# Two-layer encoder step: attention loads tied to older stores, output weights' splits spread wider, the second layer's first tile normed without a fixed place

## The chip, the cores and the metric

The kernel runs on one core of a Trainium2 chip. The metric is the device time of one execution in microseconds (us). The core has TensorE (PE: matmuls; its weight loads are shown as PEld), VectorE (DVE), ScalarE (ACT), GpSimd (POOL) and SyncE (SP), which here issues nearly all DMA transfers, in its own program order. Each engine works through its instructions in order and waits on semaphores for what the others and the DMAs produce.

## The reference

The input is 2048 prompt tokens and 64 sample tokens of width 1024. Layer A: RMS norm, one projection to q, k, v and gate, softmax attention in a band of 64-token chunks (own chunk and eight before it, learned bias), times SiLU(gate), output projection, residual. Layer B: keys and values from one projection of the stream behind layer A, q and gate from another, stick-breaking attention over all earlier keys, and the same output step; a last norm ends it. The sample tokens attend to caches as well. Cut to what matters:

```python
# layer A
q, k, v, gate = split(rms_norm(x, g_a) @ w_in_a)
x = x + (band_attend(q, k, v, rel_bias) * silu(gate)) @ w_out_a
# layer B
k, v = split(rms_norm(x, g_kv) @ w_kv)
q, gate = split(rms_norm(x, g_b) @ w_in_b)
log_fail = where(mask, log_sigmoid(-z), 0)           # z = q k^T * scale
later = reverse_cumsum(log_fail) - log_fail
w = where(mask, exp(log_sigmoid(z) + later), 0)
x = x + ((w @ v) * silu(gate)) @ w_out_b
y = rms_norm(x, g_f)
```

All in fp32, with 16 heads of 64, taken as 8 head pairs (hp).

## The kernel before, in words

Every fp32 product is three matmuls: each operand is split in a high and a low part (ACT writes the rounded high part, DVE the rest: `split`), and high x high, high x low and low x high are summed. Nearly all compute instructions go through one helper, so the profile shows them as L89 and they are told apart by their tiles.

**Stages**, in us of the profiled execution: layer A's v projection 0 to 216, its k, q and gate projections to 725, its attention to 1331, the last output tiles to 1430; layer B's v projection to 1638, its k, gate and q projections to 2036, its attention to 3191, the last output tiles to the end at about 3295.

**Projections.** `projections` norms a token tile (`turned`: load `xt`, sum of squares on ACT, `ms` on DVE, `rstd` on POOL, scaling, then eight transposes on PE to `ps_tr`), splits it to `x_own`, and multiplies it with the split v weights (`vraw` to `vwh`, `vwl`). The first two tiles and the first weights of a layer are traced with `order.on` set: then every instruction gets an edge to the one traced before it on its engine, so its place is fixed there. The others are placed by a scheduler that runs a simulated timeline over the dependences.

**What attention reads.** q, k, v and gate lie in DRAM scratch (`q_a`, `k_a`, `v_a`, `gate_a`, and `_b`). `load_q` (L475), `load_gate` (L485), `load_k` (L491), `load_v` (L500) and the `Sample` class (L516, the sample tokens' own loads `qs`, `gs`, `kt`, `vt`) issue on SyncE, as do the band bias `bias` (L1076) and the sample's `bs` (L1136). A finished block of attention output is gated and stored to `o_a` or `o_b` (L584).

**Beats and side work.** Attention runs by beats (`Beat`, L840): a beat starts one score tile (scores, softmax or stick-breaking on ACT, DVE and POOL), transposes the weights of an earlier one to `wt`, splits them to `ph` and `pl`, and multiplies an older block with the values (`acc`). Beside that the projections and output tiles that were put off are worked in steps: each beat adds a rate to an account (0.4 in A, 0.3 in B), and while it holds 1.0 or more a step runs and its cost is taken off: 1.0 for a step with matmuls, 0.5 for one without. The side work in order: late jobs (`late_job`, L701: the second half of the tokens' k, q or gate of a head pair; four in A, sixteen in B; the result `sp` or `sg` is stored in pieces, and for k rows `lkn` adds the parts back and `token_rows` transposes them by `ps_r` to the output); eight steps that load and split the output weights (`w_out_steps`, L752: `woraw` to `big`, a step without matmuls, with two splits on ACT and two on DVE); then 17 output tiles (`out_tile`: load `og` and `xr`, split to `oh` and `ol`, matmuls to `ps_o`, add, store of the new residual stream). `sp`, `sg`, `lkn` and `xr` share two buffers, so a new one waits for the stores out of the older one. What side work is left when attention ends runs alone.

**What sets the order of the loads.** SyncE issues in the order that the scheduler gives it. Loads for attention are traced well ahead of their use, and the scheduler places each when its simulated time finds its buffer free. A DMA can also wait for the landing of the one that was issued eight before it.

Of the kernel before, what the change touches and what calls it, by code (L numbers as in the profile page):

```python
# [16 lines left out]
P = 128  # L17
# [3 lines left out]
DH = 64  # L21
# [78 lines left out]
def encoder_step(ctx: ExitStack, tc: tile.TileContext, a: dict, o: dict):  # L100
# [105 lines left out]
    def put(L, kind, hp, s, cols, part):  # L206

        for i in (0, 2) if kind == "q" and s == 0 else (s,):
            nc.sync.dma_start(f32(lay[L][kind][hp][i, :, cols]), f32(part))


    def projections(L, x_of, begin, w_v, cv, gv, out_v, jobs, first, prompt, sample, stages):
        with (
# [262 lines left out]
    def load_q(L, pool, hp, h, q0):  # L476

        there(L, "q", hp, q0)
        q = pool.tile([P, 2, CH], F32R, name="q", tag="q", bufs=3 if L == "a" else 2)
        src = f32(lay[L]["q"][hp][:, h * DH : h * DH + DH, place(q0) : place(q0) + CH]).rearrange("s d t -> d s t")  # L480
        for s in range(2):
            nc.sync.dma_start(f32(q[s * DH : s * DH + DH]), src[:, s : s + 2])
        return q

    def load_gate(L, pool, hp, q0):  # L485
        there(L, "g", hp, q0)
        gt = pool.tile([P, CH], F32, name="gt", tag="gt", bufs=2)
        nc.sync.dma_start(gt, lay[L]["g"][hp][:, place(q0) : place(q0) + CH])
        return gt

    def load_k(L, hp, k0, kt):  # L491

        there(L, "k", hp, k0)
        c = place(k0) if k0 < T else k0
        for s in range(2):
            src = f32(lay[L]["k"][hp][s, :, c : c + kt.shape[2]])
            nc.sync.dma_start(f32(kt[s * DH : s * DH + DH]), src.rearrange("(h d) t -> d h t", h=2))

    def load_v(L, pool, hp, k0, n, bufs):

        tag = "vn" if n == P else "vs" if bufs == 1 else "vt"
        vt = pool.tile([P, n // P, 2, P], F32R, name="vt", tag=tag, bufs=2 if n == P else bufs)
        nc.sync.dma_start(
            f32(vt), f32(lay[L]["v"][k0 : k0 + n, 2 * hp : 2 * hp + 2]).rearrange("(j p) h c -> p j h c", p=P)
        )
        return vt
# [6 lines left out]
    class Sample:  # L513
# [9 lines left out]
        def queries(self, hp):  # L523
            q = self.q[hp % 3]
            for h in range(2):
                rows = slice(h * DH, h * DH + DH)
                src = f32(lay[self.L]["q"][hp][0:2, rows, NEW : NEW + NS])
                nc.sync.dma_start(f32(q[rows, :, rows]), src.rearrange("s d t -> d s t"))
            return q

        def gate(self, pool, hp):
            gt = pool.tile([P, NS], F32, name="gs", tag="gs", bufs=2)
            nc.sync.dma_start(gt, lay[self.L]["g"][hp][:, NEW : NEW + NS])
            return gt

        def keys_values(self, pool, hp, k0, n, bufs):
            kt = pool.tile([P, 2, n], F32R, name="kt", tag="kn" if n == NS else "kt", bufs=2 if n == NS else bufs)
            c = place(k0) if k0 < T else k0
            nc.sync.dma_start(f32(kt), f32(lay[self.L]["k"][hp][:, :, c : c + n]).rearrange("s p t -> p s t"))
# [16 lines left out]
    def gate_steps(L, pool, acc, h, c0, n, gt, sums, hp, g):  # L556
# [12 lines left out]
        def close():  # L569
            ot, tmp = sums["ot"], sums.pop(h)  # L570
            if L == "a" and n > NS:
                gps.tensor_tensor(ot[mine, :n], ot[mine, :n], tmp[mine, :n], ALU.add)
            else:
                dve.tensor_tensor(ot[mine, :n], acc()[mine, c0 : c0 + n], tmp[mine, :n], ALU.add)
            if h == 0:
                return
            if L == "b":

                t0, m = g * (CH // P), max(n // P, 1)
                by = ot[:, :n].rearrange("p (t q) -> p t q", t=m)  # L580
# [109 lines left out]
    def late_job(L, kind, w, c0, g, hp, x2, first, prompt):  # L690
# [23 lines left out]
        def out(c):  # L714
            ps = st["ps"]
            at = slice(place(HALF + c), place(HALF + c) + CH)
            if kind == "g":
                sg = opool.tile([P, CH], F32, name="sg", tag="xr", bufs=2)
                act.activation(sg, ps, AF.Sigmoid)
                dve.tensor_tensor(sg, ps, sg, ALU.mult)  # L720
                nc.sync.dma_start(lay[L]["g"][hp][:, at], sg)
            else:
                sp = opool.tile([P, 2, CH], F32R, name="sp", tag="xr", bufs=2)
                split(sp[:, 0], sp[:, 1], ps)
                for s in range(2):
                    put(L, kind, hp, s, at, sp[:, s])
                st[c] = sp
            if c + CH == HALF:
                done_late.add((L, kind, hp))
# [6 lines left out]
        def token_rows(c):  # L736
# [7 lines left out]
            nc.sync.dma_start(dst.rearrange("(j p) c -> p j c", p=P), kn[:, 1].rearrange("p (j c) -> p j c", j=4))  # L744

        chunks = range(0, HALF, CH)
        behind = []
# [92 lines left out]
    class Beat:  # L840
# [1 line left out]

        def __init__(self, lag, hold, scores_first):
            self.lag, self.hold, self.scores_first = lag, hold, scores_first
# [16 lines left out]
        def step(self):  # L863
# [60 lines left out]
        def beat(self, first=None):  # L924
# [43 lines left out]
        def end(self):  # L968
            self.rate = 1.0
            while self.tiles or self.blocks or self.held or self.marks:  # L970
                self.beat()
            order.amid = False
            while self.now or self.beside:
                self.ready = 0
                self.step()
# [47 lines left out]
    with (  # L1023
# [6 lines left out]
        banks.update(ph=4)  # L1030
        new = Sample("a", wpool)
        w_out = []
        beat = Beat(LAG["a"], HOLD["a"], True)
        beat.beside = job_steps("a", jobs_a, x2, NP - CACHE_A, o["a_k_p"])
        beat.beside += w_out_steps(a["w_out_a"][0], w_out)
        order.on = False

        def done_a(t, n, xr, c):
            if c:
                nc.sync.dma_start(x1_rows(t), xr[:n])  # L1040

        def soft_max(b, out, z, s):

# [18 lines left out]
        def items():  # L1062
            for part in ORDER:
                for hp in range(HP):
                    c0, vs = max(min(part) - 1, 0), {}
                    keys = pool.tile([P, 2, SEEN * CH], F32R, name="keys", tag="keys", bufs=2)
                    for g in part:
                        sums = {}
                        for h in range(2):
# [3 lines left out]
                                load_k("a", hp, c * CH, keys[:, :, (c - c0) * CH : (c - c0 + 1) * CH])  # L1073
                            if h == 0 and g == part[0]:
                                bias = pool.tile([P, 2, 640], F32, name="bias", tag="bias", bufs=2)
                                nc.sync.dma_start(bias, biasd[hp])  # L1076
# [52 lines left out]
        def sample_item(hp):  # L1129
            st, sums = {}, {}  # L1130

            def one():

                bs = pool.tile([P, 576], F32, name="bs", tag="bs", bufs=1)
                for h in range(2):
                    nc.sync.dma_start(bs[h * DH : h * DH + DH], biasd[hp][0:DH, h, 0:576])  # L1136
# [62 lines left out]
    with (  # L1199
# [281 lines left out]
```

## Time and profile before

| what | value |
|---|---|
| three runs | 3301.7, 3307.01, 3307.56 us (median 3307.01) |
| profiled execution | 3303.79 us |
| its span, first to last instruction | 3301.9 us |
| busy time DVE | 1922.0 us (58%) |
| busy time ACT | 1730.6 us (52%) |
| busy time POOL | 1296.1 us (39%) |
| DMA traffic | 644.37 MB, mean 195 GB/s |
| largest PE group, `ps_t<-x_own,wh` | 569.2 us of 2304 matmuls |
| `wt<-ident,s` on PE | 551.7 us of 3472 matmuls |
| `pl<-wt,ph` on DVE | 549.5 us of 864 |

A row of a timeline gives the start, the duration, the engine, the operation, what is written from what, the count, and in brackets how long the engine sat idle before it and who ended that. For a DMA the engine is SPq, and the duration is that of issuing; the landing is later. A row of stretches gives from:to, the length, the busy time of each engine with its count of instructions, the granted TensorE clock (1.00 is full), the DMA engines' share and GB/s. A piece of the chain is a start, a length and what was waited for.

### The profile page before, as it was taken

What the parts mean: (1) busy time and instruction counts of PE and PEld (TensorE: products, weight loads), DVE (VectorE), ACT (ScalarE), POOL (GpSimd) and SP (SyncE); (2) the same over time, 40 slices, a digit from 0 to 9 for tenths busy, and PEclk for the clock granted to TensorE, in tenths of its full rate; (3) what the DMA queues carried; (4) which work ended last, traced back from release to release, by engine and by line L of the source; (5) the groups of instructions that cost most, each with busy time, mean ns of one, the idle gap of its engine ahead of it and who ended that gap; (6) DMA issues with size and microseconds to landing.
All of it is one profiled execution on the core that took longest, in us unless ns stands there. A gap on an engine that the chain in (4) does not pass through costs nothing.

```text
span 3301.9 us, 53682 instructions
## 1 busy us (share of the span) xinstructions
PE 3215.2 (97%) x17928; PEld 2796.8 (85%) x17928; DVE 1922.0 (58%) x3882; ACT 1730.6 (52%) x3815; POOL 1296.1 (39%) x1950
## 2 busy tenths in 40 slices
PE   9999999999999999999999999999999999999999
PEld 7889999988888898878889999788878877888877
DVE  4234431117787777232044333899888888888873
ACT  5223322227897777143133432666666666666662
POOL 3001120005575554021044200444467776777761
PEclk9999999999899999999999999999999999999999
DMA  6359994258889894554399857777634564455423
GB/s 205 115 197 348 343 342 144 91 172 257 238 244 246 228 256 139 171 169 140 105 352 354 287 186 224 204 204 195 192 103 132 155 190 132 123 149 142 131 82 118
DMA packets 459195, 644.37 MB, mean 195 GB/s; under 512 B 49845, under 2 KB 272085, under 8 KB 458918
## 3 DMA queue, kind: packets, MB, share of 16 engines
q1 hardware_dynamic: 399462, 589.80, 57.9%
q10 hardware_dynamic: 59456, 51.13, 4.8%
q8 instruction: 143, 2.34, 0.3%
q14 instruction: 134, 1.10, 0.1%
HBM read 389.90 MB, written 250.90 MB: 194 GB/s over the span
## 4 chain that ended last, share of the span: by engine, by line
PE 77%; DVE 8%; issue 5%; DMA 4%; ACT 3%; POOL 2%; SPq 1%; POOLq 0%; DVEq 0%; ACTq 0%
PE ps_t L89 25%; PE ps_v L89 11%; PE acc L89 10%; PE ps_o L89 8%; PE z L89 8%; PE wt L89 8%; PE ps_j L89 5%; DVE s L89 3%; DVE pl L89 2%; PE ps_tr L89 1%; DVE lwl L89 1%; ACT ph L89 1%; ACT s L89 1%; POOL s L89 1%; PE ps_c L89 1%
## 5 line engine op out<-in xcount | busy, mean ns | idle before, releaser
L89 DVE TENSOR_TENSOR pl<-wt,ph 128x512 fp32r<-128x512 f32 (+1 forms) x864 | 549.5, 653 | 104.3 <-ACT ph L89 101.4
L89 ACT ACTIVATE ph<-wt 128x512 fp32r<-128x512 f32 (+1 forms) x864 | 483.2, 577 | 200.4 <-PE wt L89 191.3
L89 PE MATMUL ps_t<-x_own,wh 128*128 128x362 f32 (+1 forms) x2304 | 569.2, 327 | 0.0
L89 PE MATMUL wt<-ident,s 128*128 128x128 f32 x3472 | 551.7, 276 | 9.5 <-DVE pl L89 6.1
L89 PEld LDWEIGHTS wt<-ident,s 128*128 128x128 f32 x3472 | 421.7, 142 | 84.1 <-DVE pl L89 10.1
L89 ACT ACTIVATE f<-z 128x512 f32<-128x512 f32 (+4 forms) x680 | 355.8, 536 | 191.0 <-PE z L89 123.4
L89 POOL TENSOR_TENSOR s<-f,s 128x256 f32<-128x256 f32 x416 | 358.6, 864 | 125.7 <-DVE s L89 118.0
L89 PEld LDWEIGHTS ps_t<-x_own,wh 128*128 128x128 f32 x2304 | 405.2, 188 | 2.2
L89 PE MATMUL acc<-ph,vt 128*128 128x512 f32 (+3 forms) x1088 | 376.5, 381 | 11.4 <-ACT ph L89 5.7
L89 PE MATMUL acc<-pl,vt 128*128 128x512 f32 (+3 forms) x1088 | 367.1, 371 | 19.3 <-DVE pl L89 18.2
L89 PE MATMUL z<-kt,q 128*128 128x512 f32 (+3 forms) x1280 | 371.7, 378 | 9.6 <-ACT f L89 9.2
L89 PE MATMUL ps_t<-x_own,wl 128*128 128x362 f32 (+1 forms) x1152 | 376.6, 327 | 0.0
L89 POOL TENSOR_SCALAR s<-s,rc 128x640 f32<-128x640 f32 (+5 forms) x264 | 194.8, 744 | 427.8 <-DMA keys<-k_a 250.7
L89 PE MATMUL ps_o<-big,oh 128*128 128x512 f32 x1088 | 337.9, 394 | 0.8 <-ACT oh L89 0.5
L89 DVE TENSOR_TENSOR_SCAN s<-two,s,own 128x256 f32<-128x256 f32 x408 | 298.6, 736 | 37.8 <-POOL two L89 28.4
L89 POOL TENSOR_TENSOR two<-f 128x256 f32<-128x256 f32 x416 | 261.9, 632 | 119.6 <-ACT f L89 108.6
L89 PE MATMUL ps_t<-big,wh 128*128 128x512 f32 x896 | 278.4, 391 | 0.0
L89 PEld LDWEIGHTS z<-kt,q 128*128 128x128 f32 x1280 | 221.4, 190 | 39.9 <-ACT f L89 16.7
L89 PEld LDWEIGHTS acc<-pl,vt 128*128 128x128 f32 x1088 | 196.1, 192 | 58.8 <-DVE pl L89 44.1
L89 PEld LDWEIGHTS ps_o<-big,oh 128*128 128x128 f32 x1088 | 203.0, 189 | 42.9 <-ACT oh L89 0.9
L89 PEld LDWEIGHTS acc<-ph,vt 128*128 128x128 f32 x1088 | 198.9, 192 | 35.5 <-ACT ph L89 11.5
L89 PEld LDWEIGHTS ps_t<-x_own,wl 128*128 128x128 f32 x1152 | 216.3, 188 | 0.1
(148 smaller groups left out, 5585.0 us busy)
## 6 DMA issues: line engine op xcount, KB each, us to landing
vt<-v_b SPq DMA_DIRECT2D x80, 512.0 KB, 4.9
v_b<-vs SPq DMA_DIRECT2D x64, 512.0 KB, 5.5
q<-q_a SPq DMA_DIRECT2D x128, 256.0 KB, 5.8
q<-q_b SPq DMA_DIRECT2D x128, 256.0 KB, 4.2
vt<-v_a SPq DMA_DIRECT2D x48, 512.0 KB, 7.6
kt<-k_b SPq DMA_DIRECT2D x96, 256.0 KB, 6.2
keys<-k_a SPq DMA_DIRECT2D x80, 256.0 KB, 6.9
v_a<-vs ACTq DMA_DIRECT2D x32, 512.0 KB, 2.6
```

Source lines behind the costliest of these rows:

```text
L89: ins = op(*args, **kwargs)
```

## The change

It has three parts, and no arithmetic is changed.

1. **A queue for attention's loads.** A class `Queue` with a pace of 24 notes the attention's stores (the blocks of `o`, the late jobs' gate, q and k pieces, their token rows, and the new residual stream) with the beat in which each was traced. A load traced through it gets an edge that lets it be issued only after the newest store that is at least 24 beats old. The list is cleared when a layer's attention ends.
2. **The steps without matmuls cost more**: 1.5 in layer A and 1.0 in layer B instead of 0.5, so the eight weight steps take some 30 and 27 beats instead of some 10 and 13.
3. **The second layer's first tile**: its load and norm are traced before `order.on` is set, so their places are free; its transposes keep theirs.

```diff
+    class Queue:
+        def __init__(self, pace):
+            self.pace, self.clock, self.stores = pace, 0, []
+
+        def store(self, out, in_):
+            self.stores.append((self.clock, nc.sync.dma_start(out, in_)))
+
+        def load(self, out, in_):
+            while len(self.stores) > 1 and self.stores[1][0] <= self.clock - self.pace:
+                self.stores.pop(0)
+            behind = self.stores and self.stores[0][0] <= self.clock - self.pace
+            with tc.issue_after(self.stores[0][1].ins) if behind else nullcontext():
+                nc.sync.dma_start(out, in_)
+
+        def clear(self):
+            self.clock, self.stores = 0, []
+
+    queue = Queue(24)
...
-                def turned(t, scale=gps.tensor_scalar):
+                def normed(t, scale=gps.tensor_scalar):
                     r0, n = TOK[t]
...
                     scale(xt[:n], xt[:n], r[:n], 1.0, ALU.mult, ALU.mult)
+                    return xt
+
+                def turned(t, scale=gps.tensor_scalar, xt=None):
+                    r0, n = TOK[t]
+                    if xt is None:
+                        xt = normed(t, scale)
...
+                        xt0 = normed(seq[0], dve.tensor_scalar) if L == "b" else None
                         order.on = True
-                        tile0 = turned(seq[0], dve.tensor_scalar)
+                        tile0 = turned(seq[0], dve.tensor_scalar, xt0)
...
-            nc.sync.dma_start(f32(q[s * DH : s * DH + DH]), src[:, s : s + 2])
+            queue.load(f32(q[s * DH : s * DH + DH]), src[:, s : s + 2])
...
-            nc.sync.dma_start(lay[L]["o"][g][hp], ot[:, :n])
+            queue.store(lay[L]["o"][g][hp], ot[:, :n])
...
-            return 1.0 if product else 0.5
+            return 1.0 if product else self.blank
...
             self.clock += 1
+            queue.clock = self.clock
...
-        beat = Beat(LAG["a"], HOLD["a"], True)
+        beat = Beat(LAG["a"], HOLD["a"], True, 1.5)
...
-        beat = Beat(LAG["b"], HOLD["b"], False)
+        beat = Beat(LAG["b"], HOLD["b"], False, 1.0)
```

The other loads named above become `queue.load` in the same way, and the other stores `queue.store`.

**How the order moves.** POOL near the start of layer A's attention, as a piece of the difference (+ is after the change). `s` with its numbers are score tiles that are scaled by one over their sums, `lkn_6279` is the first add-back of a late k job:

```order
 L89 TENSOR_SCALAR s_6214<-s_6214,rc_6223 128x640
 L89 TENSOR_SCALAR s_6227<-s_6227,rc_6236 128x640
+L89 TENSOR_TENSOR lkn_6279<-sp_6258 128x512
 L89 TENSOR_SCALAR s_6240<-s_6240,rc_6255 128x640
 L89 TENSOR_SCALAR s_6264<-s_6264,rc_6276 128x640
 L89 TENSOR_SCALAR s_6282<-s_6282,rc_6302 128x640
 L89 TENSOR_SCALAR s_6310<-s_6310,rc_6337 128x640
-L89 TENSOR_TENSOR lkn_6279<-sp_6258 128x512
```

`lkn` has moved ahead of four score tiles. On SyncE at the same place the four stores of that k job, which stood behind and between the sample's loads, now stand directly behind the second `gt` load, and the sample's loads of the first head pair stand some 100 issues later.

SyncE at the start of layer B's attention, before the change. `gate_b<-sg` are the stores of the first late gate job, `gt` a gate block that attention loads, `kt` and `vt` of 64 and 512 tokens at L539 the sample's:

```order
L503 DMA vt<-v_b 128x4x256
L721 DMA gate_b_128<-sg 128x512
L482 DMA q<-q_b_111 64x2x512 x2
L488 DMA gt<-gate_b_128 128x512
L539 DMA kt<-k_b_119 128x2x64
L503 DMA vt<-v_b 128x256
L539 DMA kt<-k_b_119 128x2x512
L503 DMA vt<-v_b 128x4x256
L497 DMA kt<-k_b_120 64x2x512 x2
L721 DMA gate_b_128<-sg 128x512
```

And after it (L132 is a load, L125 a store of the queue; `q_b<-sp` are stores of the late q job):

```order
L132 DMA vt<-v_b 128x4x256
L125 DMA gate_b_128<-sg 128x512
L132 DMA q<-q_b_111 64x2x512 x2
L132 DMA gt<-gate_b_128 128x512
L125 DMA gate_b_128<-sg 128x512
L125 DMA q_b_111<-sp 128x512 x3
L132 DMA qs_21149<-q_b_111 64x2x64 x2
L132 DMA kt<-k_b_119 128x2x64
L132 DMA vt<-v_b 128x256
L132 DMA kt<-k_b_119 128x2x512
```

The second gate store and three q stores now stand ahead of the sample's loads.

DVE where layer A's last output tiles meet layer B's first tile, before the change. `xr<-ps_o` adds a product to the residual, `ms` and `xt<-xt,rstd` are steps of the norm, `vwl` the low part of the v weights:

```order
L89 TENSOR_TENSOR xr<-ps_o,ol 64x512
L89 TENSOR_TENSOR xr<-ps_o,xr 128x512 x2
L89 TENSOR_SCALAR ms<-ss 128x1
L89 TENSOR_SCALAR xt<-xt,rstd 128x1024
L89 SCALAR_TENSOR_TENSOR vwl<-vraw,g_kv,vwh 128x512 x2
L89 TENSOR_TENSOR x_own_15694<-ps_tr,x_own_15693 128x4x128 x2
```

And after it, where the norm stands:

```order
L89 TENSOR_TENSOR xr<-ps_o,xr 128x512
L89 TENSOR_SCALAR ms<-ss 128x1
L89 TENSOR_SCALAR xt<-xt,rstd 128x1024
L89 TENSOR_TENSOR ol<-og,oh 128x512 x2
L89 TENSOR_TENSOR xr<-ps_o,xr 128x512 x2
```

The two steps have moved ahead of the last nine output tiles' additions; behind the last additions `x_own` now follows without them.

More of the change, by code (lines that the diff above doesn't have):

```diff
@@ L204, in mm3, with put @@
             mm(out, sl(k), mh(k), start=False, stop=(k == NK - 1))
-    def put(L, kind, hp, s, cols, part):
+    def put(L, kind, hp, s, cols, part, by=nc.sync.dma_start):
         for i in (0, 2) if kind == "q" and s == 0 else (s,):
-            nc.sync.dma_start(f32(lay[L][kind][hp][i, :, cols]), f32(part))
+            by(f32(lay[L][kind][hp][i, :, cols]), f32(part))
     def projections(L, x_of, begin, w_v, cv, gv, out_v, jobs, first, prompt, sample, stages):
@@ L487, in load_gate @@
         gt = pool.tile([P, CH], F32, name="gt", tag="gt", bufs=2)
-        nc.sync.dma_start(gt, lay[L]["g"][hp][:, place(q0) : place(q0) + CH])
+        queue.load(gt, lay[L]["g"][hp][:, place(q0) : place(q0) + CH])
         return gt
@@ L496, in load_k @@
             src = f32(lay[L]["k"][hp][s, :, c : c + kt.shape[2]])
-            nc.sync.dma_start(f32(kt[s * DH : s * DH + DH]), src.rearrange("(h d) t -> d h t", h=2))
+            queue.load(f32(kt[s * DH : s * DH + DH]), src.rearrange("(h d) t -> d h t", h=2))
     def load_v(L, pool, hp, k0, n, bufs):
@@ L502, in load_v @@
         vt = pool.tile([P, n // P, 2, P], F32R, name="vt", tag=tag, bufs=2 if n == P else bufs)
-        nc.sync.dma_start(
+        queue.load(
             f32(vt), f32(lay[L]["v"][k0 : k0 + n, 2 * hp : 2 * hp + 2]).rearrange("(j p) h c -> p j h c", p=P)
@@ L527, in queries @@
                 src = f32(lay[self.L]["q"][hp][0:2, rows, NEW : NEW + NS])
-                nc.sync.dma_start(f32(q[rows, :, rows]), src.rearrange("s d t -> d s t"))
+                queue.load(f32(q[rows, :, rows]), src.rearrange("s d t -> d s t"))
             return q
@@ L532, in gate @@
             gt = pool.tile([P, NS], F32, name="gs", tag="gs", bufs=2)
-            nc.sync.dma_start(gt, lay[self.L]["g"][hp][:, NEW : NEW + NS])
+            queue.load(gt, lay[self.L]["g"][hp][:, NEW : NEW + NS])
             return gt
@@ L538, in keys_values @@
             c = place(k0) if k0 < T else k0
-            nc.sync.dma_start(f32(kt), f32(lay[self.L]["k"][hp][:, :, c : c + n]).rearrange("s p t -> p s t"))
+            queue.load(f32(kt), f32(lay[self.L]["k"][hp][:, :, c : c + n]).rearrange("s p t -> p s t"))
             r0, m = (k0 - NS * (self.L == "b"), P) if n == NS else (k0, n)
@@ L720, in out @@
                 dve.tensor_tensor(sg, ps, sg, ALU.mult)
-                nc.sync.dma_start(lay[L]["g"][hp][:, at], sg)
+                queue.store(lay[L]["g"][hp][:, at], sg)
             else:
@@ L725, in out @@
                 for s in range(2):
-                    put(L, kind, hp, s, at, sp[:, s])
+                    put(L, kind, hp, s, at, sp[:, s], queue.store)
                 st[c] = sp
@@ L743, in token_rows @@
             dst = prompt[b : b + CH, hp * P : hp * P + P]
-            nc.sync.dma_start(dst.rearrange("(j p) c -> p j c", p=P), kn[:, 1].rearrange("p (j c) -> p j c", j=4))
+            queue.store(dst.rearrange("(j p) c -> p j c", p=P), kn[:, 1].rearrange("p (j c) -> p j c", j=4))
         chunks = range(0, HALF, CH)
@@ L840, in encoder_step, with __init__ @@
     class Beat:
-        def __init__(self, lag, hold, scores_first):
-            self.lag, self.hold, self.scores_first = lag, hold, scores_first
+        def __init__(self, lag, hold, scores_first, blank):
+            self.lag, self.hold, self.scores_first, self.blank = lag, hold, scores_first, blank
             self.clock = 0
@@ L972, in end @@
             order.amid = False
+            queue.clear()
             while self.now or self.beside:
@@ L1039, in done_a @@
             if c:
-                nc.sync.dma_start(x1_rows(t), xr[:n])
+                queue.store(x1_rows(t), xr[:n])
         def soft_max(b, out, z, s):
@@ L1075, in items @@
                                 bias = pool.tile([P, 2, 640], F32, name="bias", tag="bias", bufs=2)
-                                nc.sync.dma_start(bias, biasd[hp])
+                                queue.load(bias, biasd[hp])
                             for c in fresh:
@@ L1135, in one @@
                 for h in range(2):
-                    nc.sync.dma_start(bs[h * DH : h * DH + DH], biasd[hp][0:DH, h, 0:576])
+                    queue.load(bs[h * DH : h * DH + DH], biasd[hp][0:DH, h, 0:576])
                 q = new.queries(hp)
```

## The prediction

> **What bounds the kernel now.** I read first the span with its clock, then the busy shares, then busy time and granted clock in short stretches, then who waits for whom in the stretches that fall out.
>
> The first fence is the span and mean TensorE clock of the core, the second TensorE's row of busy times on the page.
>
> ```profile
> core 0: 3301.9 us, clock 0.992
> ```
>
> ```profile
> PE 3215.2 (97%) x17928; PEld 2796.8 (85%) x17928; DVE 1922.0 (58%) x3882; ACT 1730.6 (52%) x3815; POOL 1296.1 (39%) x1950
> ```
>
> TensorE (PE) bounds it: 3301.9 - 3215.2 = 86.7 us of idle, and a mean clock of 0.992 costs at most 0.008 x 3301.9 = 26 us more. No matmul is added or removed, so all that the change can win lies in these 113 us. The next rows are five stretches: length, busy time of PE, PEld, DVE, ACT and POOL, then the granted clock, the DMA share and GB/s.
>
> ```profile
> 757.00:765.00 8.00, 7.32 (x37) 6.66 (x36) 4.14 (x13) 5.59 (x14) 2.68 (x5) 0.56 1.02 261
> 882.00:908.00 26.00, 21.58 (x118) 19.55 (x116) 19.62 (x50) 21.03 (x49) 12.39 (x16) 0.77 0.74 216
> 1026.00:1035.00 9.00, 6.73 (x28) 5.46 (x27) 5.09 (x14) 6.87 (x16) 4.19 (x5) 0.81 1.04 271
> 1430.00:1440.00 10.00, 7.62 (x34) 5.93 (x34) 7.92 (x14) 7.15 (x14) 3.25 (x5) 0.83 0.78 262
> 2065.00:2075.00 10.00, 8.89 (x39) 7.29 (x39) 9.36 (x17) 7.61 (x19) 6.34 (x12) 0.68 0.94 272
> ```
>
> A mean of 0.83 over 10 us is 2 x 0.17 x 10 = 3.4 us at half clock; the others give 7.0, 12.0, 3.4 and 6.4 us. Each follows an idle of PE that is shown below, and each costs up to half its length. The change touches four of the five places on purpose and the third by what it moves. The profiled execution took 3303.79 us, 1.9 over its span; the runs shown are 3301.7, 3307.01 and 3307.56, the mean of all four 3305.0, which is 1.2 over the profiled run and 2.0 under the median. The sum is made on the profiled run and its result carried over to that mean. About 0.2%, 6.6 us, can be told from no change.
>
> **The change part by part.**
>
> *Queue, first layer's start.* SyncE's issues (start, time, line), then POOL, PE and ACT rows of the same place, each with the idle before it and its releaser, and the matching pieces of the chain; the last row is the load's time from issue to landing.
>
> ```profile
> 739.67 2.40 SPq L488 DMA_DIRECT2D gt<-gate_a  x1
> ...
> 748.64 0.32 SPq L209 DMA_DIRECT2D k_a<-sp  x1
> ```
>
> ```profile
> 744.74 0.81 POOL L89 TENSOR_SCALAR s<-s,rc 128x640 f32<-128x640 f32 x1 [0.44 <-DVE rc L89]
> ```
>
> ```profile
> 754.80 1.26 POOL L89 TENSOR_TENSOR lkn<-sp 128x512 f32<-128x512 f32 x1 [7.07 <-DMA vt<-v_a]
> ```
>
> ```profile
> 746.26 0.38 PE L89 MATMUL wt<-ident,s 128*128 128x128 f32 x2
> ```
>
> ```profile
> 756.11 1.11 PE L89 MATMUL ps_r<-ident,lkn 128*128 128x128 f32 x4 [4.71 <-POOL lkn L89]
> ```
>
> ```profile
> 759.62 1.97 PE L89 MATMUL wt<-ident,s 128*128 128x128 f32 x8 [0.68 <-ACT lkn L89]
> ```
>
> ```profile
> 748.64 6.02 DMA k_a<-sp
> ```
>
> ```profile
> 756.04 2.33 DMA k_a<-sp
> ```
>
> ```profile
> gt<-gate_a SPq DMA_DIRECT2D x1, 256.0 KB, 9.8
> ```
>
> The late k job's stores wait in SyncE's order behind the sample's loads; `lkn` takes the buffer of the first pair, so POOL waits 7.07 us and PE 4.71 + 0.68 = 5.39 us. After the change all four stores stand directly behind the gt load, so the first goes out at 739.67 + 2.40 = 742.1, and the others right behind it, where the second of the first pair went out at 748.64 and the last at 756.04. They are behind that load's bytes, which land at 739.7 + 9.8 = 749.5; I let the first pair land at 750.3 and 751.0, 3.7 us earlier than the 754.7 of the chain. But the same change moves `lkn` on POOL ahead of four `s` of the 128x640 kind, and PE needs those early: it transposed such tiles at 746.26, and comes to them at about 745.4 with four of the eight z matmuls ahead of them moved behind. `lkn` would run 751.0 to 752.3, one `s` (0.81) later PE resumes at 753.1: 7.7 us idle in the place of 5.39, with the second wait gone. The half clock behind it stays. I take +1.5; ends -9 (stores land at once, below) and +4 (a later landing).
>
> *Queue, first layer's middle.* The sample's loads of its first head pair, 1.5 MB (bs, qs, kt, vt), leave 745 and now stand before the pair of og loads, at about 975 to 990. A wait that this lengthens, and the stretch's DMA share (1.06):
>
> ```profile
> 1027.48 0.63 ACT L89 ACTIVATE oh<-og 128x512 fp32r<-128x512 f32 x1 [2.53 <-DMA og<-o_a]
> ```
>
> ```profile
> 1028.65 0.50 PE L89 MATMUL acc<-ph,vt 128*128 128x384 f32 x2 [1.78 <-ACT ph L89]
> ```
>
> ```profile
> 1005.00:1026.00 21.00, 20.49 (x136) 18.84 (x135) 15.24 (x38) 14.08 (x31) 10.16 (x11) 1.00 1.06 259
> ```
>
> At 259 GB/s 1.5 MB are 5.8 us of a full queue. Against it, two keys loads (0.5 MB, 2 us) now stand behind the second og instead of before it. og comes perhaps 2 us later; every later load has some 24 beats of slack. I take +1.5 (-2 to +5).
>
> *Queue, second layer's start.* Issues, the chain, ACT, PE, and the landing time of the gt load:
>
> ```profile
> 2047.87 0.59 SPq L488 DMA_DIRECT2D gt<-gate_b  x1
> ...
> 2056.86 0.34 SPq L721 DMA_DIRECT2D gate_b<-sg  x1
> ```
>
> ```profile
> 2047.18 9.60 DMA q<-q_b
> ```
>
> ```profile
> 2056.86 8.09 DMA gate_b<-sg
> ```
>
> ```profile
> 2064.97 0.60 ACT L89 ACTIVATE sp<-ps_j 128x512 fp32r<-128x512 f32 x1 [5.30 <-DMA gate_b<-sg]
> ```
>
> ```profile
> 2066.11 1.22 PE L89 MATMUL z<-kt,q 128*128 128x512 f32 x2 [5.34 <-ACT f L89]
> ```
>
> ```profile
> gt<-gate_b SPq DMA_DIRECT2D x1, 256.0 KB, 9.5
> ```
>
> The second gate store goes out at 2056.86, behind sample loads, lands 8.09 us later, and `sp`, which needs its buffer, holds the `f` behind it on ACT: PE waits 5.34 us and then has 6.4 us of half clock. After the change the store stands next behind gt: issue about 2049, landing with gt (2047.9 + 9.5 = 2057.4) or just after, 2058.2, before ACT comes to `sp` at about 2059. The idle goes (5.3) and most of the clock loss (3.2): -8.5, less 1 for what is late next, since SyncE then waits for the q job's `sp` with the sample's and the next pair's kt loads behind it. I take -7.5 (-9 to -4). The rest of the second layer's loads moves by less than their lead: 0 (-2 to +3).
>
> *w_out splits, first layer.* Eight steps of two splits on ACT and two on DVE, now one step per 3.75 beats instead of 1.25 (cost 1.5 or 0.5 at a rate of 0.4). ACT's groups in 857 to 908, then in the 97 us behind:
>
> ```profile
> L89 ACT ACTIVATE s<-s,mn 128x640 f32<-128x640 f32 (+4 forms) x24 | 15.9, 664 | 0.0
> ```
>
> ```profile
> L89 ACT ACTIVATE big<-woraw 128x512 fp32r<-128x512 f32 x16 | 9.2, 624 | 1.9 <-DMA woraw<-in_w_out_a 1.9
> ```
>
> ```profile
> L89 ACT ACTIVATE s<-s,mn 128x640 f32<-128x640 f32 (+4 forms) x62 | 44.6, 723 | 0.9 <-DVE mn L89 0.8
> ```
>
> 24 score tiles in 51 us, then 62 in 97: 1.565 us each without splits. Before: 148 us. After: ACT stays the bound there, so 86 x 1.565 + 9.2 / 0.95 = 144.3. The gain is not the whole loss of 13.4 us, only the waits for woraw and the half clock: -4 (-8 to +1). Out tiles do not start before the og loads at about 995, so none is delayed.
>
> *w_out splits, second layer.* The `f` on ACT in two stretches, with splits and without side work, then DVE there (third busy time) and its splits:
>
> ```profile
> 2700.00:2735.00 35.00, 8.27 (x15) 1.00 0.81 260
> ```
>
> ```profile
> 3100.00:3190.00 90.00, 33.55 (x62) 1.00 0.42 117
> ```
>
> ```profile
> 2700.00:2735.00 35.00, 27.46 (x148) 20.06 (x147) 33.86 (x55) 24.74 (x52) 26.61 (x40) 1.00 0.81 260
> ```
>
> ```profile
> 3100.00:3190.00 90.00, 85.26 (x487) 67.07 (x486) 80.61 (x131) 64.57 (x130) 75.05 (x143) 1.00 0.42 117
> ```
>
> ```profile
> L89 DVE TENSOR_TENSOR big<-woraw,big 128x512 fp32r<-128x512 f32 x16 | 13.3, 864 | 1.0 <-ACT big L89 1.0
> ```
>
> One `f` a beat: 2.33 us with splits, DVE 97% busy; 1.45 without. 13 beats become 27 (8 / 0.3), taken from the end's beats without side work. Before 13 x 2.33 + 14 x 1.45 = 50.6; after, bound by DVE, 27 x (80.61 / 62 + 13.3 / 27) / 0.97 = 49.9: -1 (-4 to +2). DVE's work does not shrink, so spreading it wins little.
>
> *Second layer's first tile.* The out tiles' last 10 us, the norm's POOL step, and the transposes:
>
> ```profile
> 1420.00:1430.00 10.00, 9.79 (x44) 7.77 (x42) 1.81 (x4) 1.92 (x4) 0.00 (x0) 1.00 0.44 130
> ```
>
> ```profile
> 1430.71 0.56 POOL L89 TENSOR_TENSOR rstd<-ms,nhalf 128x1 f32<-128x1 f32 x1 [97.25 <-DVE ms L89]
> ```
>
> ```profile
> 1432.16 1.09 PE L89 MATMUL ps_tr<-ident,xt 128*128 128x128 f32 x8 [2.37 <-issue]
> ```
>
> The norm now stands some 20 additions earlier on DVE, in the out tiles' tail, where PE hides it: DVE is busy for 1.81 of 10 us there, ACT for 1.92. (Without that cover its steps would cost PE the 2.37 us as now.) The tile's rows were stored long before. PE goes straight to the transposes: 2.2 of the 2.37 us, and the 3.4 us of half clock cost 1.7, of which I give 1.3: -3.5 (-4.2 to -1.5). The Trainium skill, TensorE: Matmul & The Clock Gate, Part 1, says that the clock halves after at least one idle window of about 3.4 us; by it 2.37 us would not do, and the edit would be worth 2.2 alone. The trace disagrees: 0.83 here and 0.81 after the 1.78 us at 1028.65; I go by the rows.
>
> Sum: 1.5 + 1.5 - 7.5 - 4 - 1 - 3.5 = -13: 3303.79 - 13 = 3290.8 on the profiled run, and 3305.0 - 13 = **3292** us beside the mean.
>
> **The rivals.** *The stores land on their own* (0.10). The store at 756.04 landed in 2.33 us with loads still under way. If the first layer's do so too, they land by 745, `lkn` delays nobody, 5.39 us of idle and some 3 of the clock loss go: -8.4 instead of +1.5, 3282. Against it: 6.02 and 8.09 us for the others. The Trainium skill, DMA: Bandwidth & Descriptors, Queues, rings and completion order, says that completion is not in the order of issue, which allows it; only the run can tell.
>
> *The waits only change hands* (0.24). SyncE still issues in one order. If the queue's fuller places (1.06) hold the same engines for other transfers, the second layer's start gives -2, the first layer's splits -1, the first tile -2.2, the rest +3: 3303. For it speaks the lane on which SyncE waited 9.60 us for q before it could issue the gate store.
>
> *Lone splits are bursts: slower* (0.12). Packed, 16 steps lose 13.4 us in the first layer and 35 - 15 x 1.45 = 13.3 in the second. Apart, each could hold ACT's in-order stream for 2 x 0.62 = 1.25 us and drop the clock for 3.4 us, worth 1.7: 16 x 2.95 = 47.2 less 26.7 is +20.5. With the other terms (-8) that is 3317.5. It turns slower once a lone step costs over (26.7 + 8) / 16 = 2.2 us. For it: the 1.78 us idle that alone brought 0.81. Against: clock 1.00 all through 2700 to 2735.
>
> **How the numbers follow.** My forecast has 0.54: 3292, by itself 3283 to 3300 (ends of unlike terms seldom meet). To hold 8 in 10 the range takes in most of the first two rivals and leaves out the slower one and the tails: 3280 to 3306. Faster is under about 3300: nearly all of mine (0.49), the first rival (0.10), two fifths of the second (0.10): 0.69. Slower is over about 3313: most of the third and a little of the second, 0.10. Same is 0.21.
>
> **What would show it.** Right: no `sp` wait on the gate store near 2060 and a clock near 1.0 there; ps_tr of the second layer's first tile with under 0.3 us idle; first layer's splits over some 70 us with less half clock; `lkn` still the releaser of PE's longest wait near 750. Wrong: a lone split followed by idle PE at reduced clock; ACT waiting for gate_b as before; no wait near 750 (first rival); og waits well over 5 us.

## The result, and the profile after

The changed kernel took 3324.85 us (median of four runs, 3319.98 to 3328.36), the kernel before 3304.36 us (four runs, 3300.29 to 3307.56): a ratio of 1.006, 95% interval 1.0048 to 1.0072. It is 20.5 us slower. The forecast was 3292 us, in a range from 3280 to 3306: wrong in its sign. The profiled execution after took 3328.36 us, its span 3326.6.

PE's row of the page after, then the row of the core:

```profile
PE 3221.1 (97%) x17928; PEld 2799.0 (84%) x17928; DVE 1928.9 (58%) x3882; ACT 1735.2 (52%) x3815; POOL 1305.5 (39%) x1950
```

```profile
core 0: 3326.6 us, clock 0.991
```

The two profiled executions' spans are 24.7 us apart. PE has the same matmuls; its idle went from 86.7 to 105.5 us, and it is busy for 5.9 us longer, at a mean clock of 0.991 for 0.992. Where, is told by the start of the n-th instruction of a kind in both traces. The first rows count ACT's instructions on softmax tiles of layer A (`s<-s,mn`, two a tile), the row `ps_v` the first multiplications of layer B's projection, the others ACT's `f` on the score tiles of layer B's attention:

```
                 before      after - before
A  softmax  32    769.4 us      -0.7
A  softmax 160    906.0         -7.9
A  softmax 288   1006.7         -3.0
A  softmax 320   1053.2         -0.1
A  softmax 512   1291.6         +3.0
B  ps_v    300   1454.4         +0.4
B  f         0   2054.0         -0.3
B  f        12   2073.4         -5.1
B  f        96   2205.1         -1.4
B  f       144   2280.8         +9.5
B  f       180   2340.3        +13.9
B  f       204   2376.6        +21.5
B  f       384   2690.6        +21.6
B  f       432   2781.4        +18.5
B  f       672   3179.9        +24.1
```

Between f 96 and f 204, in some 180 us, 22.9 us are lost. That is nearly the whole loss; what lies before and behind it sums to 1.8 us. PE's longest waits from 2040 to 2420 us, before and then after (who waited for whom: total, times, longest):

```profile
PE z L89 <- ACT f L89: 5.3, 1, 5.3
```

```profile
PE z L89 <- DMA q<-q_b: 19.2, 6, 5.6
```

In the kernel before no q load was waited for there. Four of the six q waits, 15.1 us, lie between f 96 and f 204, and a stretch of half clock goes with each. With the two longest it is 6.8 us, at 0.50 from end to end:

```profile
2254.75:2261.57 6.82, 4.77 (x16) 4.12 (x17) 1.81 (x3) 1.37 (x3) 0.00 (x0) 0.50 0.49 99
2387.87:2394.70 6.83, 4.01 (x13) 3.55 (x14) 2.43 (x5) 1.55 (x4) 0.00 (x0) 0.50 0.36 99
```

With the other two it is 3.4 us each (from 2210.38 and 2343.49, PE busy throughout). PE is busy for 15.6 us of the four stretches; an estimate, at half of that, is 7.8 us lost, and with the 15.1 us of waits this is the 22.9. Before, the clock is 1.00 from 2200 to 2420. SyncE's issues around one of those waits, before:

```profile
2215.67 1.23 SPq L482 DMA_DIRECT2D q<-q_b  x2
2216.95 2.63 SPq L497 DMA_DIRECT2D kt<-k_b  x4
2219.62 0.59 SPq L539 DMA_DIRECT2D kt<-k_b  x1
2220.26 1.22 SPq L528 DMA_DIRECT2D qs<-q_b  x2
2223.80 0.33 SPq L584 DMA_DIRECT2D o_b<-ot  x1
```

And after:

```profile
2217.93 1.24 SPq L132 DMA_DIRECT2D q<-q_b  x2
2226.05 0.33 SPq L125 DMA_DIRECT2D o_b<-ot  x1
2226.42 0.42 SPq L132 DMA_DIRECT2D gt<-gate_b  x1
2226.90 1.24 SPq L132 DMA_DIRECT2D qs<-q_b  x2
2228.18 0.59 SPq L132 DMA_DIRECT2D kt<-k_b  x1
2228.87 1.23 SPq L132 DMA_DIRECT2D q<-q_b  x2
2230.14 0.59 SPq L132 DMA_DIRECT2D vt<-v_b  x1
2230.78 0.43 SPq L132 DMA_DIRECT2D kt<-k_b  x1
2231.26 0.47 SPq L132 DMA_DIRECT2D vt<-v_b  x1
2231.77 1.28 SPq L132 DMA_DIRECT2D kt<-k_b  x2
2233.09 0.81 SPq L132 DMA_DIRECT2D vt<-v_b  x1
2233.95 1.75 SPq L132 DMA_DIRECT2D kt<-k_b  x2
2235.79 0.54 SPq L132 DMA_DIRECT2D vt<-v_b  x1
```

Before, the next head pair's keys went out ahead of the `o_b` store, in SyncE's time before that store's block was ready. After, SyncE stands idle from 2219.2 to 2226.05 for that store's block, and everything tied behind it goes out in the 10 us that follow: fifteen loads, 4.1 MB (1.5 MB of keys and 1.5 MB of values in pieces of 256 and 512 KB, 0.5 of q, 0.25 of gate, and the sample's small ones). The chain shows what that does to the next q load, and PE's row the wait, each from the profile after:

```profile
2235.04 14.02 DMA kt<-k_b
2249.08 7.58 DMA q<-q_b
```

```profile
2256.80 0.66 PE L89 MATMUL z<-kt,q 128*128 128x128 f32 x2 [4.80 <-DMA q<-q_b]
```

The second half of q waits for the landing of the kt load issued eight DMAs before it (its lane; 14.02 us after issue), then 7.58 us for itself. The chains of the waits at 2210 and 2391 us have the same form. Its own turn comes only when one of its two buffers is free, so it has no lead to lose.

The stretches that the prediction showed, after the change, and ahead of them the one behind the first wait of layer A:

```profile
749.47:756.30 6.83, 5.79 (x22) 5.27 (x22) 2.66 (x8) 3.19 (x7) 4.39 (x7) 0.50 0.55 139
```

```profile
757.00:765.00 8.00, 7.73 (x58) 7.03 (x57) 6.98 (x23) 7.04 (x20) 2.86 (x6) 1.00 0.51 145
882.00:908.00 26.00, 20.95 (x132) 18.72 (x130) 22.88 (x62) 23.98 (x56) 17.64 (x19) 0.93 0.91 271
...
1026.00:1035.00 9.00, 6.20 (x22) 5.21 (x23) 4.79 (x14) 6.88 (x16) 3.21 (x4) 0.62 1.07 288
1430.00:1440.00 10.00, 9.43 (x46) 6.50 (x45) 5.80 (x9) 6.74 (x13) 2.38 (x3) 1.00 0.67 214
...
2065.00:2075.00 10.00, 6.92 (x34) 4.57 (x34) 9.60 (x17) 6.76 (x16) 6.51 (x13) 1.00 1.07 285
```

Three of the five now have a better clock, as was meant. The stretch from 757 has 1.00 only because its half clock has moved ahead of it, as the first row shows. The one with og has a worse one: 0.62, not 0.81.

### The profile page after: what moved, and what is told of

Read it like the earlier page. It is cut to its first block, busy times and chain, and to the rows that moved or that the text cites. A ratio compares the mean times of both kernels' runs of the same rounds, so it can differ in the third digit from the quotient of the medians.

```text
span 3326.6 us, 53711 instructions
## 1 busy us (share of the span) xinstructions
PE 3221.1 (97%) x17928; PEld 2799.0 (84%) x17928; DVE 1928.9 (58%) x3882; ACT 1735.2 (52%) x3815; POOL 1305.5 (39%) x1950
## 4 chain that ended last, share of the span: by engine, by line
PE 73%; DVE 8%; issue 7%; DMA 6%; ACT 3%; POOL 1%; SPq 1%; POOLq 0%; DVEq 0%; ACTq 0%
PE ps_t L89 25%; PE ps_v L89 11%; PE acc L89 10%; PE z L89 8%; PE wt L89 8%; PE ps_o L89 6%; PE ps_j L89 5%; DVE s L89 3%; DVE pl L89 3%; DMA q<-q_b 1%; DMA kt<-k_b 1%; ACT ph L89 1%; ACT s L89 1%; SPq L132 1%; PE ps_tr L89 1%
## 5 line engine op out<-in xcount | busy, mean ns | idle before, releaser
L89 DVE TENSOR_TENSOR_SCAN s<-f,own 128x128 f32<-128x128 f32 (+4 forms) x264 | 201.9, 787 | 43.5 <-ACT f L89 35.0
```

Of the source, the lines that this page charges most:

```text
L89: ins = op(*args, **kwargs)
```

## The experiments

Each result is the ratio to the kernel before, timed beside it, with its 95% interval. The edits are shown against the changed kernel, cut to what differs.

**Which edit.** Three kernels have one edit each, a fourth has all three but the edges in layer A only. Theory: the loss is the edges' in layer B. Rivals: it needs the spread splits, or lone splits are bursts.

The norm alone (no edges, steps without matmuls at 0.5):

```diff
-    queue = Queue(24)
+    queue = Queue(10**6)
...
-        beat = Beat(LAG["a"], HOLD["a"], True, 1.5)
+        beat = Beat(LAG["a"], HOLD["a"], True, 0.5)
...
-        beat = Beat(LAG["b"], HOLD["b"], False, 1.0)
+        beat = Beat(LAG["b"], HOLD["b"], False, 0.5)
```

> Only the second layer's first tile is normed without a fixed place; no store edges, weight steps at 0.5. Theory (each edit's effect is local, and the loss comes from the store edges in the second layer): the wait of 2.37 us ahead of ps_tr and the half clock behind it go, -2.6 us as between the two traces there, so 0.999 of before. Rival (moving the norm shifts the scheduler's order further on and costs there): over 1.002.

Measured: 0.9995 (0.9985 to 1.0004). From softmax 512 to `ps_v` 300 its trace is 2.6 us shorter, as expected; so small a gain is inside the interval.

The costs of 1.5 and 1.0 alone:

```diff
-    queue = Queue(24)
+    queue = Queue(10**6)
...
-                        xt0 = normed(seq[0], dve.tensor_scalar) if L == "b" else None
+                        xt0 = None
```

> Only the output weights' steps cost 1.5 and 1.0. Theory (store edges cause the loss): -2 us in the first layer, -3 us at the second layer's splits and up to +5 behind them, so within 5 us of before, 0.9985 to 1.0015. Rival (lone splits are bursts, the slower rival of the prediction): +12 us or more, over 1.003.

Measured: 0.9983 (0.9974 to 0.9993), a little faster, and just under the range expected. The rival of the bursts falls.

The edges alone:

```diff
-                        xt0 = normed(seq[0], dve.tensor_scalar) if L == "b" else None
+                        xt0 = None
...
-        beat = Beat(LAG["a"], HOLD["a"], True, 1.5)
+        beat = Beat(LAG["a"], HOLD["a"], True, 0.5)
...
-        beat = Beat(LAG["b"], HOLD["b"], False, 1.0)
+        beat = Beat(LAG["b"], HOLD["b"], False, 0.5)
```

> Only the store edges, in both layers. Theory: the whole loss is here: about +25 us in the second layer between 2200 and 2400 us with PE waiting for q, -5 at that layer's start, +5 in the first layer's late and middle places: 1.006 to 1.009. Rival (the edges do harm only together with the spread splits): within 5 us of before.

Measured: 1.0065 (1.0049 to 1.0081). Its trace gains 5.3 us at the start of layer B and loses 19.8 between f 96 and f 204, with 17.1 us of waits for q. The loss is all the edges'.

All three edits, the edges ended with layer A:

```diff
         def clear(self):
-            self.clock, self.stores = 0, []
+            self.pace, self.clock, self.stores = 10**6, 0, []
```

> All three edits, but the store edges in the first layer only. Theory: without the second layer's edges the PE waits for q go, and so does the gain at that layer's start: before +0 at 2050 us, then -3 to +3: 0.998 to 1.001. Rival (the q waits of 2200 to 2400 us come from the spread splits or the late jobs' shifted times): still over 1.004.

Measured: 0.9985 (0.9975 to 0.9995), in the expected range. The edges do their harm in layer B.

**Why q waits.** Two theories. Bunch: keys and values that an edge holds back go out together behind one `o_b` store, and q queues behind them. Hold: q's own edge ties it to a store that is late. In the next two kernels layer B's edges are taken from one set of loads; in layer A they stay.

```diff
+    def by(L, tied=False):
+        return queue.load if L == "a" or tied else nc.sync.dma_start
...
-            queue.load(f32(kt[s * DH : s * DH + DH]), src.rearrange("(h d) t -> d h t", h=2))
+            by(L)(f32(kt[s * DH : s * DH + DH]), src.rearrange("(h d) t -> d h t", h=2))
...
-        queue.load(
+        by(L)(
             f32(vt), f32(lay[L]["v"][k0 : k0 + n, 2 * hp : 2 * hp + 2]).rearrange("(j p) h c -> p j h c", p=P)
```

and the same for the sample's loads; only the prompt's q and gate keep the edges.

> The full change, but in the second layer only q and gate loads of the prompt keep the edges; key, value and all sample loads are free as before. Theory B (bunch: key and value loads held back by an edge all go out right behind one o_b store, and q, which has two buffers and no lead, queues behind their bytes): no PE wait for q over 2 us between 2200 and 2400, the 25 us gone, 0.997 to 1.001. Rival H (the hold itself: q waits for its own edge's store): the waits for q stay, over 1.004.

Measured: 0.9987 (0.9977 to 0.9996). PE's longest waits from 2040 to 2420:

```profile
PE acc L89 <- DVE pl L89: 5.3, 10, 1.0
PE z L89 <- ACT f L89: 3.9, 1, 3.9
```

No q wait is left, so q's own edge alone is not the cause. The 3.9 us are the gate store's stall at the start, shorter than before's.

The other way round, q and gate free, the rest tied:

```diff
-            queue.load(f32(q[s * DH : s * DH + DH]), src[:, s : s + 2])
+            by(L)(f32(q[s * DH : s * DH + DH]), src[:, s : s + 2])
...
-        queue.load(gt, lay[L]["g"][hp][:, place(q0) : place(q0) + CH])
+        by(L)(gt, lay[L]["g"][hp][:, place(q0) : place(q0) + CH])
```

> The full change, but in the second layer q and gate loads of the prompt are free and the key, value and sample loads keep the edges. Theory B: q still queues behind the bunch, PE waits 10 us or more for q between 2200 and 2400, 1.004 to 1.008. Rival H: the waits go, under 1.001.

Measured: 1.0057 (1.0036 to 1.0078), with the waits back:

```profile
PE z L89 <- DMA q<-q_b: 17.1, 5, 6.3
```

The bunch it is. Whose loads, asked the next kernel: only the sample's are free (and its values, by a flag to `load_v`).

```diff
-                queue.load(f32(q[rows, :, rows]), src.rearrange("s d t -> d s t"))
+                by(self.L)(f32(q[rows, :, rows]), src.rearrange("s d t -> d s t"))
...
-            queue.load(f32(kt), f32(lay[self.L]["k"][hp][:, :, c : c + n]).rearrange("s p t -> p s t"))
+            by(self.L)(f32(kt), f32(lay[self.L]["k"][hp][:, :, c : c + n]).rearrange("s p t -> p s t"))
```

> The full change, but in the second layer the sample's loads (qs, gs, kt and vt of the sample and its cache) are free, the prompt's q, gate, keys and values keep the edges. Theory B with the sample's cache as most of the bunch (three pairs of 512 KB each at 2228 to 2236): most of the 25 us gone, under 1.002. If the prompt's own keys and values make the bunch: over 1.004. Rival H: over 1.004.

Measured: 0.9982 (0.9974 to 0.9991); no q wait. One count of that expectation was wrong: of the three pairs of 512 KB only one is the sample's, the others are the next head pair's. SyncE at that place, where L570 and L559 are lines of freed loads:

```profile
2209.50 1.25 SPq L132 DMA_DIRECT2D q<-q_b  x2
2210.84 0.55 SPq L570 DMA_DIRECT2D kt<-k_b  x1
2212.19 1.23 SPq L559 DMA_DIRECT2D qs<-q_b  x2
2217.63 0.33 SPq L125 DMA_DIRECT2D o_b<-ot  x1
2218.01 0.43 SPq L132 DMA_DIRECT2D gt<-gate_b  x1
2218.50 1.23 SPq L132 DMA_DIRECT2D kt<-k_b  x2
2219.95 0.42 SPq L132 DMA_DIRECT2D vt<-v_b  x1
2220.47 1.23 SPq L132 DMA_DIRECT2D q<-q_b  x2
2221.75 1.25 SPq L132 DMA_DIRECT2D kt<-k_b  x2
```

The sample's keys and q go ahead of the store again, and with what is left of the bunch no q is late.

**What of the gain at layer B's start.** Here the edges hold only in layer B's first 40 beats, with both other edits:

```diff
-            behind = self.stores and self.stores[0][0] <= self.clock - self.pace
+            behind = self.on and self.clock < 40 and self.stores and self.stores[0][0] <= self.clock - self.pace
...
-            self.clock, self.stores = 0, []
+            self.clock, self.stores, self.on = 0, [], True
```

> Spread splits, free norm, and the store edges only in the second layer's first 40 beats, none in the first layer. Theory B with local effects: -3.4 us before 2050 and -2.6 for the norm, -5 at the second layer's start, no q waits later, -1 for its splits: 12 us less than before, 0.9955 to 0.9975. Rival (the gain at that start is given back later, as it was in part in the run with edges in both layers): 0.998 or more.

Measured: 0.9979 (0.997 to 0.9988), between the two and nearer to the rival. The 5.0 us of the first 12 `f` come, and 3.8 go again by f 24, with a q wait behind the first bunch, the one that follows the gate store and the late q job's stores:

```profile
2065.58 0.66 PE L89 MATMUL z<-kt,q 128*128 128x128 f32 x2 [4.22 <-DMA q<-q_b]
```

**Has q no lead?** The full change, with a third q buffer in layer B:

```diff
-        q = pool.tile([P, 2, CH], F32R, name="q", tag="q", bufs=3 if L == "a" else 2)
+        q = pool.tile([P, 2, CH], F32R, name="q", tag="q", bufs=3)
```

> The full change with three q buffers instead of two in the second layer. Theory B says that q is hit because it has no lead, not because it is q: with one more buffer a q load can go out one unit of work earlier, and the waits of PE for q between 2040 and 2420 (19 us in the change) fall under 6 us: 0.998 to 1.002. Rival (the bunch's bytes, 14 us on a lane and 8 in the queue, outlast any such lead): the waits stay over 12 us, over 1.003.

Measured: 0.9974 (0.9964 to 0.9984), better than the range expected. The bunches are still there (fifteen loads from 2210.67 to 2220.93), but no q is waited for, and the 5 us at the start stay. PE's longest wait, then the stretch of the loss in this kernel and in the change:

```profile
PE acc L89 <- DVE pl L89: 5.6, 12, 1.0
```

```profile
2200.00:2420.00 220.00, 214.40 (x1257) 180.81 (x1256) 197.13 (x340) 150.87 (x338) 112.24 (x195) 1.00 0.69 186
```

```profile
2200.00:2420.00 220.00, 200.63 (x1138) 169.95 (x1137) 178.79 (x311) 134.57 (x304) 92.40 (x156) 0.95 0.68 179
```

In these 220 us the change gets through 1138 of PE's instructions, this kernel through 1257, with the DMA engines as busy. The same buffer alone (the edit against the kernel before):

```diff
-        q = pool.tile([P, 2, CH], F32R, name="q", tag="q", bufs=3 if L == "a" else 2)
+        q = pool.tile([P, 2, CH], F32R, name="q", tag="q", bufs=3)
```

> The kernel before with three q buffers in the second layer and nothing else. Theory: q is not waited for there before, so within 0.1% of before, 0.999 to 1.001. Rival (the third buffer, not the end of the bunch's harm, made the gain of the run with all edits and three buffers): under 0.998.

Measured: 1.0011 (1.0001 to 1.0021), a shade slower and just over the range expected: without the bunches the buffer brings nothing.

**Edges where they gain.** Both other edits, no edges in layer A, in layer B edges for all but the sample's loads:

```diff
+    def by(L, tied=False):
+        return queue.load if L == "b" and tied else nc.sync.dma_start
...
-            behind = self.stores and self.stores[0][0] <= self.clock - self.pace
+            behind = self.on and self.stores and self.stores[0][0] <= self.clock - self.pace
...
-            queue.load(f32(kt), f32(lay[self.L]["k"][hp][:, :, c : c + n]).rearrange("s p t -> p s t"))
+            by(self.L)(f32(kt), f32(lay[self.L]["k"][hp][:, :, c : c + n]).rearrange("s p t -> p s t"))
```

`on` is set when layer A's attention has ended, and the sample's other loads go through `by` as well.

> Spread splits and the free norm, no edges in the first layer, and in the second layer edges for all loads but the sample's. Theory: the first layer as in the run with 40 beats (-9 to -12 us at 2054), a further -2.5 at the second layer's start as in the run with the sample's loads free, no q waits: 0.9955 to 0.998, not over the run with 40 beats. Rival (edges on the prompt's loads cost in the second layer without the first layer's): over 0.999.

Measured: 0.997 (0.9959 to 0.9981), about 10 us faster than before. With the third q buffer as well:

```diff
-        q = pool.tile([P, 2, CH], F32R, name="q", tag="q", bufs=3 if L == "a" else 2)
+        q = pool.tile([P, 2, CH], F32R, name="q", tag="q", bufs=3)
```

> Spread splits, free norm, no edges in the first layer, in the second layer edges for all but the sample's loads, and three q buffers there. Theory: the third buffer only covers what the bunch did; without the bunch it brings nothing more: within 2 us of the run without it, 0.996 to 0.998. Rival (the lead of q is worth something by itself): under 0.996.

Measured: 0.9982 (0.9973 to 0.9991). The buffer brings nothing on top; the intervals of the last two kernels and of the change with three q buffers overlap, and which is best stays open.

## Why the prediction was wrong, point by point

**The step that failed** is "The rest of the second layer's loads moves by less than their lead: 0 (-2 to +3)". It measured +22.9 between f 96 and f 204, and +3.7 between f 12 and f 96. The step took the 24 beats as a lead that all the loads have, and looked at each load alone. But in SyncE's one order an edge is a gate: when its store is not ready, SyncE stands (6.9 us above), and what was tied goes out at once. What matters then is the lead of whatever issues next, and q's is one buffer. The prediction had the number that warns, the 9.60 us that a q load took in a crowded queue, and quoted it for the gate store's sake. It had even named who queues behind SyncE's wait at the start ("the sample's and the next pair's kt loads"), charged 1 us for it, and not asked whether that repeats at each head pair.

**First layer's start, +1.5.** The mechanism was right, the sizes were not. POOL and PE after:

```profile
748.41 1.26 POOL L89 TENSOR_TENSOR lkn<-sp 128x512 f32<-128x512 f32 x1 [8.49 <-DMA k_a<-sp]
```

```profile
750.51 0.69 PE L89 MATMUL wt<-ident,s 128*128 128x128 f32 x2 [5.51 <-POOL s L89]
```

`lkn` does hold the `s` tiles behind it, for 5.5 us and not 7.7. The half clock stayed, as forecast: 6.83 us of it from 749.47, where before it was 10.24 from 753.81. At softmax 32 the sum is unchanged from the first tile: 0, not +1.5. The first rival, stores that land on their own, did not come: the chain has 8.10 us for this store.

**First layer's middle, +1.5.** Right in kind: og took 9.62 us, not 6.86.

```profile
1017.81 9.62 DMA og<-o_a
```

```profile
1028.61 0.80 PE L89 MATMUL acc<-ph,vt 128*128 128x384 f32 x2 [4.60 <-ACT ph L89]
```

PE waits 4.60 us for it, not 1.78, and the clock is 0.62, not 0.81: 2.9 us from softmax 288 to 320. Yet the kernel with the costs alone, without any edge, has a wait of 3.5 us there too, so not all of it can be put down to the moved loads.

**Second layer's start, -7.5.** The mechanism came as written: the second gate store went out at 2048.80 (2056.86 before), and ACT took the `sp` behind it at 2058.71 without a wait:

```profile
2058.71 0.59 ACT L89 ACTIVATE sp<-ps_j 128x512 fp32r<-128x512 f32 x1
```

The size was 4.8, and the first bunches took 3.7 of it back by f 96.

**Splits, -4 and -1.** Layer A: -7.2 us from softmax 32 to 160, -2.6 when the splits are over; the splits took 51 us (868 to 919), not some 70. Layer B: -3.1 from f 384 to 432, then +5.6 to f 672. Of these, 3.2 come behind f 608, where output tiles now run (the last product of them at 3127, before at 3085); the prediction gave this move no price. So layer B's term is +2.5 in this pair. The kernel with the costs alone has the same two moves (-3.5 and +5.5), and by its ten executions the splits of both layers together gain 0.17%, 5.6 us, while its one trace shows 1.3. It refutes the rival of lone splits.

**First tile, -3.5.** -2.6, from softmax 512 to `ps_v`. No wait ahead of the transposes is left, and the clock is 1.00, not 0.83:

```profile
1432.60 1.04 PE L89 MATMUL ps_tr<-ident,xt 128*128 128x128 f32 x8
```

The half clock before went together with a wait of 2.37 us, against the rule of the Trainium skill, TensorE: Matmul & The Clock Gate, Part 1 (a whole idle window of some 3.4 us); the trace decides.

**The rivals.** "The waits only change hands" had the right culprit, SyncE's one order, but no place and no price for it: it ended at 3303. The slower rival had the wrong mechanism.

## What to carry to other kernels

An edge that makes loads wait for a store does not only order them: where one engine issues all transfers in order, it turns each late store into a gate with a bunch behind it. Before tying loads, sum the bytes that stand in a row in the new order (here 4.1 MB in 10 us), divide by the rate (an estimate: 19 us at the 219 GB/s from 2226 to 2250), and compare that with the lead of the load that has the fewest buffers, not with the lead of the loads that are tied. No run tested this sum as a rule, nor told apart what the wait on the lane and the bytes in the queue each cost q; what was tested are two cures, and each alone was enough: leaving the sample's loads free (0.9982) or one more buffer for the load that is hit (0.9974). Choose the windows of a clock reading by the waits, too: from 757 to 765 the half clock of layer A's start seems gone, and it only lies ahead.

## What the runs showed of the hardware

The half clock comes with waits well under 3 us too, and its length goes with the wait's only roughly. Two stretches of the kernel before, behind waits of 1.78 and 2.37 us:

```profile
1030.29:1033.70 3.41, 3.41 (x12) 2.83 (x11) 2.78 (x8) 3.35 (x10) 2.17 (x3) 0.50 1.09 259
1433.06:1436.47 3.41, 3.19 (x9) 2.38 (x8) 3.08 (x6) 3.41 (x7) 0.04 (x1) 0.50 0.97 359
```

After the change the waits of 4.60, 4.80, 5.51 and 5.62 us each go with 6.83 us of half clock, those of 1.79 and 2.89 us for q with 3.41, but those of 2.21 and 1.83 us, ended at 2075 and 2168, with none: the clock is 1.00 there. All of these lengths are one or two times 3.41 us.

Whether it comes is not fixed by the program either. The stretch of layer B's splits in the kernel before, then in the kernel with the free norm alone, whose program is the same there:

```profile
2690.00:2760.00 70.00, 62.20 (x347) 48.99 (x345) 64.81 (x103) 48.20 (x101) 50.12 (x84) 1.00 0.63 186
```

```profile
2690.00:2760.00 70.00, 61.79 (x322) 49.88 (x321) 60.72 (x99) 46.06 (x94) 47.42 (x82) 0.90 0.64 182
```

One execution has a full clock there, the other 2 x 0.10 x 70 = 14 us of half clock, and falls 4.3 us behind in the splits. In layer A the kernels with free keys, with q and gate free, with the sample free and with three q buffers have the change's program; against before they stand at -1.1, -4.8, -3.0 and -5.4 us at softmax 352 to 368, the change itself at -0.2. From softmax 32 to 256, across the splits, the five read -2.5 to -7.3. So a term of less than 5 us, read from one pair of traces, has no firm size, and the three small terms in layer A can't be settled one by one.
